# Spreading eight bias rows over 128 partitions in a decoder trunk: four skewed DRAM writes from SBUF against one DRAM to DRAM copy and one read

## The chip, the core and the metric

One core of one Trainium2 chip runs the whole program. The metric is the time of one execution in device microseconds (us); lower is better. The kernel before took 974.55 us, the median of three runs (974.48, 974.55 and 975.95).

## The reference

A two-layer decoder trunk over 256 tokens of width 1024. Each layer is a half-step SwiGLU feed-forward (width 2816), a mixer (differential attention, a short convolution and a gated recurrence side by side, one projection in and one out), and a second half-step feed-forward. Only one piece of it matters here, the relative bias of the attention:

```python
dist = q_pos[:, None] - k_pos[None, :]
bias = rel_bias[t5_bucket(jnp.maximum(dist, 0))]
...
logits = jnp.einsum('bqhmd,bkhmd->bhmqk', qb, k).astype(f32) + bias
logits = jnp.where(dist >= 0, logits, NEG_INF)
```

The bias of one of the eight maps (4 heads, 2 maps each) depends on the distance q - k alone. So a row of 384 numbers holds all of a map: row q of the bias is that row read from a place shifted by q.

## The kernel before, in words

All weights are float32 and are streamed from DRAM once, in 167 pieces of mostly 512 KB, in one fixed list. `load` (L143) issues a piece's DMA on SP into one of six `raw` buffers. `high` (L159) lets ScalarE (ACT) write the piece's float32r part `wh`, `low` (L164) lets VectorE (DVE) write the rest `wl`; `wh` and `wl` have seven buffers each. When `low` has freed a `raw` buffer, the next piece is loaded (`low_to`, L168). TensorE (PE) multiplies with `wh` and `wl` in three products (`mm3`, L203), which stand in the profile as L204, L205 and L206.

The first feed-forward runs `up_gate` (L300): 11 units (`c` from 0 to 10), each of four pieces and 48 matmuls of 128x512 into two PSUM banks `na` and `nb`. At the end of a unit `gate` (L313) lets ACT apply Silu (`sg`, L317) and DVE multiply (`ga`, L319). During the next unit `turn` (L324) transposes `ga` on PE (`hT`, four matmuls of L328), and ACT and DVE copy the result into `hid` (L330, L331). Then `ffn` (L374) runs the down projection (L221, L222) over 22 more pieces.

Each engine runs its instructions in the order in which they are written; a DMA is issued by the sequencer of the engine that it is written on, and what stands behind it there waits until the issue is through. At the end of a unit, after `gate`, `up_gate` calls a hook (L371). The dictionary `once` (L826 to L829) puts the setup of the mixer there:

- hook 1, `constants_in`: small loads on ACT's queue. Hook 2, `bias_rows` (L456): one matmul and a copy make `br`, 8 rows of 384 floats on 8 partitions of SBUF.
- hooks 3 to 6, `skew_out(0)` to `skew_out(3)` (L462): each writes two rows of `br`, each 128 times, into the DRAM scratch `skew`, laid out [8, 128, 384].
- hooks 7 to 10, `skew_in(0)` to `skew_in(3)` (L470): each reads two maps back into `bias` (128 partitions, 8, 256), partition p from an address that moves by 383 floats and not 384, which makes the shift. The first reader of `bias` is the attention of the mixer (L541), after the whole down projection.

The DMAs of SP and ACT share eight completion semaphores, DMAHW0 to DMAHW7, which are given out in turn in the order of the program. A DMA is issued only when the one before it on the same semaphore has landed. With hardly any DMAs but the loads, a load thus waits for the DMA written eight places before it.

Of the kernel before, what the change touches and what calls it, by code (L numbers as in the profile page):

```python
# [11 lines left out]
F32 = mybir.dt.float32  # L12
# [5 lines left out]
P = 128  # L18
DEPTH = 2
S = 256  # L20
# [50 lines left out]
def trunk(ctx: ExitStack, tc: tile.TileContext, t, out):  # L71
    nc = tc.nc
# [7 lines left out]
    dr = ctx.enter_context(tc.tile_pool(name="dr", bufs=1, space=bass.MemoryType.DRAM))  # L80
# [28 lines left out]
    bias = cst.tile([P, 8, S], F32, name="bias")  # L109
# [264 lines left out]
    def ffn(norm, first, gain, hooks=()):  # L374
        hid, last = up_gate(norm, first, hooks)
        for n in range(4):
            acc = pair("d")
            for k0, k1 in DOWN_K:
                w = take(1)[0]
                for i in range(2):  # L380
                    c = slice(i * P, (i + 1) * P)
                    for k in range(k0, k1):
                        wide(acc[i], w[0][:, k - k0, c], w[1][:, k - k0, c], hid[k], k == 0, k == KF - 1)
                    if k1 == KF:
                        settle(2 * n + i, acc[i], gain, True)
                done(1)
                if n == 0 and k0 == 8:
                    last()
                pump()


    kept = {}
# [66 lines left out]
        kept["br"] = wk.tile([8, 384], F32, tag="at", name="br")  # L459
        nc.vector.tensor_copy(out=kept["br"], in_=b[:8, :384])  # L460

    def skew_out(i):  # L462

        if i == 0:
            kept["skew"] = dr.tile([8, P, 384], F32, name="skew")
        m = slice(2 * i, 2 * i + 2)
        rows_ = kept["br"][m].unsqueeze(1).to_broadcast([2, P, 384])
        nc.scalar.dma_start(out=kept["skew"][m], in_=rows_)

    def skew_in(i):  # L470
        sk = kept["skew"][:]
        nc.scalar.dma_start(
            out=bias[:, 2 * i:2 * i + 2],
            in_=bass.AP(sk.tensor, sk.offset + 2 * i * P * 384 + P - 1, [[383, P], [P * 384, 2], [1, S]]),
        )


    def mixer(l, norm):
# [344 lines left out]
        nc.vector.tensor_tensor(out=xq, in0=junk[:, 0], in1=junk[:, 1], op=ALU.add)  # L823

    norm = Norm()
    once = {1: constants_in, 2: bias_rows, 3: exponents, 4: softplus, 5: factors}  # L826
    for i in range(4):
        once[3 + i] = (lambda i, old: lambda: (old and old(), skew_out(i)))(i, once.get(3 + i))
        once[7 + i] = lambda i=i: skew_in(i)  # L829
    ffn(norm, True, ("mix_norm", 0), once)  # L830
    for l in range(DEPTH):
        norm = Norm()
# [126 lines left out]
```

## Time and profile before

| what | value |
|---|---|
| median of three runs | 974.55 us |
| the profiled execution, whole | 974.53 us |
| its span (first to last instruction) | 972.4 us |
| PE busy in it | 956.2 us (98%) |
| DVE, ACT busy | 582.4 us (60%), 508.1 us (52%) |
| mean granted TensorE clock | 0.994 |
| moved by DMA | 176.64 MB, 171.46 MB of it on SP's queue (q1), 4.30 MB on ACT's (q10) |

The span is the sum to compare with; 2.1 us lie around it. Two of the page's lines, in 40 slices of 24.3 us each, show where the kernel is uneven: PEclk is the granted TensorE clock in tenths of full speed, and DMA the busy share of the 16 DMA engines in tenths.

| line | slices 0 to 39 |
|---|---|
| PEclk | 9999989999999999999999999999999999999999 |
| DMA | 8854465644346555555555455556434455555621 |

Slice 5 (121.6 to 145.9 us) is the only one with a clock digit under 9.

### The profile page before, as it was taken

The numbers are of one execution on the slowest core, as the hardware profiler recorded it, in microseconds if no ns is written. First come the engines' busy times: TensorE is split into PE (matmuls) and PEld (weight loads), VectorE is DVE, ScalarE is ACT, GpSimd is POOL, SyncE is SP. The second block draws the span as 40 slices with busy tenths as digits, with TensorE's granted clock in tenths as the row PEclk, the third lists the DMA queues.
The fourth block names the chain that finished last, engine by engine and source line by source line (L and its number), as shares of the span: only waits on it lengthen the run. The fifth ranks groups of instructions, "written<-read, shape, count | busy, mean of one in ns | idle before, by whom it ended". The sixth has DMA issues, their size and how long they took to land.

```text
span 972.4 us, 13915 instructions
## 1 busy us (share of the span) xinstructions
PE 956.2 (98%) x5350; PEld 831.9 (86%) x5350; DVE 582.4 (60%) x812; ACT 508.1 (52%) x775; POOL 24.1 (2%) x46
## 2 busy tenths in 40 slices
PE   9999889999999999999999999999999999999997
PEld 7788668899999888888888888888999988888886
DVE  6665355567787555555655555565778765555543
ACT  7564244457775554444445444454678655444441
POOL 0011000000000000000000000000000000000000
PEclk9999989999999999999999999999999999999999
DMA  8854465644346555555555455556434455555621
GB/s 307 292 181 150 155 238 186 205 164 163 131 174 206 189 200 183 178 172 188 174 215 179 174 189 183 163 188 222 160 136 161 163 210 197 176 174 189 220 89 44
DMA packets 53045, 176.64 MB, mean 182 GB/s; under 512 B 6867, under 2 KB 8948, under 8 KB 52980
## 3 DMA queue, kind: packets, MB, share of 16 engines
q1 hardware_dynamic: 48960, 171.46, 51.4%
q10 hardware_dynamic: 4020, 4.30, 1.5%
q8 instruction: 42, 0.69, 0.3%
q14 instruction: 23, 0.19, 0.1%
HBM read 173.11 MB, written 2.62 MB: 181 GB/s over the span
## 4 chain that ended last, share of the span: by engine, by line
PE 90%; DMA 7%; issue 1%; ACT 1%; DVE 1%; SPq 0%; ACTq 0%; POOLq 0%; POOL 0%; DVEq 0%
PE na L204 7%; PE nb L204 7%; PE na L206 7%; PE na L205 7%; PE nb L206 7%; PE nb L205 7%; PE db L221 6%; PE da L221 6%; DMA skew<-br 3%; DMA raw<-in_ffn_gu 3%; PE da L222 3%; PE db L222 3%; PE hT L328 2%; PE v L204 1%; PE wb L206 1%
## 5 line engine op out<-in xcount | busy, mean ns | idle before, releaser
L162 ACT ACTIVATE wh<-raw 128x1024 fp32r<-128x1024 f32 (+1 forms) x334 | 340.3, 1031 | 292.9 <-PE nb L206 102.8
L166 DVE TENSOR_TENSOR wl<-raw,wh 128x1024 fp32r<-128x1024 f32 (+1 forms) x334 | 388.5, 1187 | 77.9 <-ACT wh L162 77.9
L204 PE MATMUL na<-wh,xx 128*128 128x512 f32 x352 | 142.4, 404 | 0.6 <-ACT wh L162 0.6
L205 PE MATMUL na<-wl,xx 128*128 128x512 f32 x352 | 138.2, 393 | 0.2 <-DVE wl L166 0.2
L206 PE MATMUL na<-wh,xx 128*128 128x512 f32 x352 | 138.4, 393 | 0.0
L204 PE MATMUL nb<-wh,xx 128*128 128x512 f32 x352 | 137.8, 391 | 0.0
L206 PE MATMUL nb<-wh,xx 128*128 128x512 f32 x352 | 137.4, 390 | 0.0
L205 PE MATMUL nb<-wl,xx 128*128 128x512 f32 x352 | 137.2, 390 | 0.0
L331 DVE TENSOR_TENSOR hid<-hT,hid 128x512 fp32r<-128x512 f32 x44 | 30.4, 691 | 133.1 <-ACT hid L330 133.1
L221 PE MATMUL da<-hid,wh 128*128 128x512 f32 x252 | 92.3, 399 | 0.0
L221 PE MATMUL db<-hid,wh 128*128 128x512 f32 x252 | 92.1, 398 | 0.0
L206 PEld LDWEIGHTS na<-wh,xx 128*128 128x128 f32 x352 | 66.6, 189 | 14.4
L204 PEld LDWEIGHTS nb<-wh,xx 128*128 128x128 f32 x352 | 66.5, 189 | 13.9
L205 PEld LDWEIGHTS nb<-wl,xx 128*128 128x128 f32 x352 | 66.4, 189 | 14.0
L204 PEld LDWEIGHTS na<-wh,xx 128*128 128x128 f32 x352 | 66.8, 190 | 13.5 <-ACT wh L162 1.5
L206 PEld LDWEIGHTS nb<-wh,xx 128*128 128x128 f32 x352 | 66.2, 188 | 14.1
L205 PEld LDWEIGHTS na<-wl,xx 128*128 128x128 f32 x352 | 66.9, 190 | 13.0 <-DVE wl L166 0.8
L222 PE MATMUL da<-hid,wl 128*128 128x256 f32 x252 | 70.7, 280 | 0.0
L222 PE MATMUL db<-hid,wl 128*128 128x256 f32 x252 | 70.6, 280 | 0.0
L330 ACT ACTIVATE hid<-hT 128x512 fp32r<-128x512 f32 x44 | 26.3, 599 | 79.7 <-PE hT L328 79.7
L319 DVE SCALAR_TENSOR_TENSOR ga<-na,rr,sg 128x256 f32<-128x256 f32 x44 | 21.2, 483 | 76.7 <-ACT sg L317 76.7
L221 PEld LDWEIGHTS db<-hid,wh 128*128 128x128 f32 x252 | 47.4, 188 | 11.2
(282 smaller groups left out, 1520.8 us busy)
## 6 DMA issues: line engine op xcount, KB each, us to landing
raw<-in_ffn_gu SPq DMA_DIRECT2D x172, 512.0 KB, 4.4
raw<-in_ffn_down SPq DMA_DIRECT2D x82, 512.0 KB, 4.2
raw<-in_w_in SPq DMA_DIRECT2D x44, 512.0 KB, 4.5
raw<-in_w_out SPq DMA_DIRECT2D x16, 512.0 KB, 4.8
raw<-in_ffn_down SPq DMA_DIRECT2D x12, 256.0 KB, 2.7
raw<-in_ffn_gu SPq DMA_DIRECT2D x8, 256.0 KB, 5.5
skew<-br ACTq DMA_DIRECT2D x4, 384.0 KB
xT<-in_x SPq DMA_DIRECT2D x4, 256.0 KB, 5.7
```

What stands on the lines that cost most here:

```text
L162: nc.scalar.activation(out=parts[i][0][:, s], in_=raws[i][:, s], func=AF.Copy)
L166: nc.vector.tensor_tensor(out=lo[:, s], in0=raws[i][:, s], in1=h[:, s].bitcast(F32), op=ALU.subtract)
L204: nc.tensor.matmul(o, lhsT=ah, rhs=bh, start=first, stop=False)
L205: nc.tensor.matmul(o, lhsT=ah, rhs=bl, start=False, stop=False)
L206: nc.tensor.matmul(o, lhsT=al, rhs=bh, start=False, stop=last)
L221: nc.tensor.matmul(o, lhsT=wh, rhs=flat(v), start=first, stop=False)
L222: nc.tensor.matmul(o[:, :S], lhsT=wl, rhs=v[:, 0], start=False, stop=False)
L319: nc.vector.scalar_tensor_tensor(out=a[:, k], in0=b[k][:, 256:], scalar=norm.r[:, k:k + 1], in1=s[:, k], op0=ALU.mult, op1=ALU.mult)
L328: nc.tensor.transpose(b[:, (2 * j + k) * P:(2 * j + k + 1) * P], a[:, k, tok(j)], ident)
L330: nc.scalar.activation(out=h[:, :, 0], in_=two(b), func=AF.Copy)
L331: nc.vector.tensor_tensor(out=h[:, :, 1], in0=two(b), in1=h[:, :, 0].bitcast(F32), op=ALU.subtract)
```

## The change

The row buffer `br` goes out to a small DRAM buffer `rows` as it is (hook 6). A second DMA copies that buffer 128 times within DRAM into `skew`, now laid out [128, 8, 384] (hook 8). A third reads all of `bias` back at once, partition p from an address that moves by 8 x 384 - 1 floats (hook 10). All three stay on ACT's queue. Eight DMAs become three; hooks 7 and 9 are gone, and hooks 3, 4 and 5 keep only the arithmetic that they had.

```diff
-    def skew_out(i):
-
-        if i == 0:
-            kept["skew"] = dr.tile([8, P, 384], F32, name="skew")
-        m = slice(2 * i, 2 * i + 2)
-        rows_ = kept["br"][m].unsqueeze(1).to_broadcast([2, P, 384])
-        nc.scalar.dma_start(out=kept["skew"][m], in_=rows_)
-
-    def skew_in(i):
+    def rows_out():
+        kept["rows"] = dr.tile([8, 384], F32, name="rows")
+        nc.scalar.dma_start(out=kept["rows"], in_=kept["br"])
+
+    def skew_out():
+
+        kept["skew"] = dr.tile([P, 8, 384], F32, name="skew")
+        r = kept["rows"][:]
+        nc.scalar.dma_start(out=kept["skew"], in_=bass.AP(r.tensor, r.offset, [[0, P], [384, 8], [1, 384]]))
+
+    def skew_in():
         sk = kept["skew"][:]
-        nc.scalar.dma_start(
-            out=bias[:, 2 * i:2 * i + 2],
-            in_=bass.AP(sk.tensor, sk.offset + 2 * i * P * 384 + P - 1, [[383, P], [P * 384, 2], [1, S]]),
-        )
+        nc.scalar.dma_start(out=bias, in_=bass.AP(sk.tensor, sk.offset + P - 1, [[8 * 384 - 1, P], [384, 8], [1, S]]))
...
-    once = {1: constants_in, 2: bias_rows, 3: exponents, 4: softplus, 5: factors}
-    for i in range(4):
-        once[3 + i] = (lambda i, old: lambda: (old and old(), skew_out(i)))(i, once.get(3 + i))
-        once[7 + i] = lambda i=i: skew_in(i)
+    once = {
+        1: constants_in, 2: bias_rows, 3: exponents, 4: softplus, 5: factors, 6: rows_out, 8: skew_out, 10: skew_in
+    }
```

Three places show how the instructions move. The number behind a name only tells one buffer from another, and "waits" names the semaphores that an instruction waits for.

The first is ACT's queue at the end of unit 8. Before:

```order
L317 ACTIVATE sg<-na,rr 128x256
L317 ACTIVATE sg<-nb,rr 128x256
L472 DMA bias<-skew 128x2x256
L162 ACTIVATE wh_1070<-raw_959 128x1024 [waits DMAHW0_49,DVE_49,PE_49]
L330 ACTIVATE hid_124<-hT 128x2x256 [waits PE_49]
```

Now:

```order
L317 ACTIVATE sg<-na,rr 128x256
L317 ACTIVATE sg<-nb,rr 128x256
L470 DMA skew<-rows 128x3072 [waits DMAHW0_49]
L162 ACTIVATE wh_1067<-raw_956 128x1024 [waits DMAHW4_49,DVE_49,PE_49]
L330 ACTIVATE hid_124<-hT 128x2x256 [waits PE_49]
```

The read of two maps has given way to the copy within DRAM, which waits for the copy of `rows` that was issued two units earlier.

The second is ACT's queue at the end of unit 10, the last of `up_gate`. Before:

```order
L317 ACTIVATE sg<-nb,rr 128x256
L472 DMA bias<-skew 128x2x256
L162 ACTIVATE wh_1250<-raw_1135 128x1024 [waits DMAHW1_49,DVE_49,PE_49]
L162 ACTIVATE wh_1272<-raw_1162 128x1024 [waits DMAHW3_49,DVE_49,PE_49]
L330 ACTIVATE hid_125<-hT 128x2x256 [waits PE_49]
```

Now:

```order
L317 ACTIVATE sg<-nb,rr 128x256
L474 DMA bias<-skew 128x8x256 [waits DMAHW1_49]
L162 ACTIVATE wh_1246<-raw_1132 128x1024 [waits DMAHW5_49,DVE_49,PE_49]
L162 ACTIVATE wh_1268<-raw_1158 128x1024 [waits DMAHW6_49,DVE_49,PE_49]
L330 ACTIVATE hid_125<-hT 128x2x256 [waits PE_49]
```

One read of all eight maps stands there now; it waits for the copy within DRAM (DMAHW1), and the high parts of the next pieces and the last `hid` stand behind it.

The third is SP's queue, where a load takes over the semaphore of a slow DMA. Before, the loads written eight places behind the writes of `skew`:

```order
L151 DMA raw_773<-in_ffn_gu 128x1024 [waits DMAHW6_49,DVE_49]
L151 DMA raw_810<-in_ffn_gu 128x1024 [waits DMAHW7_49,DVE_49,Activation_49]
L151 DMA raw_835<-in_ffn_gu 128x1024 [waits DMAHW0_49,DMAHW1_49,DVE_49,Activation_49]
L151 DMA raw_853<-in_ffn_gu 128x1024 [waits DMAHW2_49,DVE_49]
L151 DMA raw_871<-in_ffn_gu 128x1024 [waits DMAHW3_49,DVE_49]
L151 DMA raw_898<-in_ffn_gu 128x1024 [waits DMAHW4_49,DMAHW5_49,DVE_49,Activation_49]
```

Now, the eighth load behind the copy within DRAM, which has DMAHW1 (with `raw_1219`):

```order
L151 DMA raw_1158<-in_ffn_down 128x1024 [waits DMAHW7_49,DVE_49,Activation_49]
L151 DMA raw_1183<-in_ffn_down 128x1024 [waits DMAHW0_49,DVE_49,Activation_49]
L151 DMA raw_1201<-in_ffn_down 128x1024 [waits DMAHW2_49,DVE_49]
L151 DMA raw_1219<-in_ffn_down 128x512 [waits DMAHW3_49,DMAHW1_49,DVE_49]
L151 DMA raw_1250<-in_ffn_down 128x1024 [waits DMAHW4_49,DVE_49,Activation_49]
```

The loads still wait for ACT's DMAs eight places back, but in the gate and up pieces of units 4 to 10 no write of `skew` stands there any more.

## Rows read from the trace of the kernel before

**Rows 1.** The page, busy time of each engine, its share and instructions.

```profile
PE 956.2 (98%) x5350; PEld 831.9 (86%) x5350; DVE 582.4 (60%) x812; ACT 508.1 (52%) x775; POOL 24.1 (2%) x46
```

**Rows 2.** Waits of PE, whole span: total us, times, longest us.

```profile
PE hT L328 <- DVE ga L319: 8.3, 3, 5.6
```

**Rows 3.** Timeline of PE: start us, us; in brackets idle before.

```profile
107.07 1.29 PE L328 MATMUL hT<-ident,ga 128*128 128x128 f32 x4 [2.33 <-DVE ga L319]
108.02 0.78 PE L204 MATMUL na<-wh,xx 128*128 128x512 f32 x1
...
126.03 1.29 PE L328 MATMUL hT<-ident,ga 128*128 128x128 f32 x4 [5.57 <-DVE ga L319]
126.97 0.78 PE L204 MATMUL na<-wh,xx 128*128 128x512 f32 x1
```

**Rows 4.** Chain that ended last, 30 to 240 us: start us, us, what.

```profile
70.69 0.44 PE hT L328 x4
...
76.77 33.27 DMA skew<-br
...
112.52 11.41 DMA raw<-in_ffn_gu
124.04 0.46 ACT wh L162
...
140.14 0.44 PE hT L328 x4
...
237.02 0.64 PE sc L539 x4
```

**Rows 5.** The same chain in the second feed-forward.

```profile
334.12 0.44 PE hT L328 x4
...
345.47 0.44 PE hT L328 x4
```

**Rows 6.** Windows: length, PE, PEld, DVE, ACT, POOL busy (count); PEclk; DMA share; GB/s.

```profile
87.00:92.00 5.00, 5.00 (x24) 4.14 (x23) 3.71 (x5) 1.79 (x3) 0.00 (x0) 1.00 0.11 29
...
102.00:107.00 5.00, 2.74 (x13) 1.93 (x11) 1.69 (x3) 2.85 (x4) 0.00 (x0) 1.00 0.13 51
107.00:112.00 5.00, 4.86 (x16) 3.89 (x17) 1.54 (x3) 0.00 (x0) 0.00 (x0) 0.66 0.26 59
...
127.00:132.00 5.00, 5.00 (x15) 4.00 (x14) 2.32 (x3) 1.15 (x2) 0.00 (x0) 0.57 0.69 232
132.00:137.00 5.00, 5.00 (x23) 4.13 (x22) 3.21 (x4) 3.36 (x5) 0.00 (x0) 1.00 1.03 412
...
905.00:910.00 5.00, 5.00 (x28) 4.32 (x27) 3.22 (x4) 2.84 (x4) 0.00 (x0) 1.00 0.87 305
```

**Rows 7.** Waits of SP's queue, 92 to 130 us: total us, times, longest us.

```profile
SPq L151 <- DMA skew<-br: 35.4, 3, 12.4
```

**Rows 8.** Timeline of SP, pieces around a pause in the loads.

```profile
81.31 0.33 SPq L151 DMA_DIRECT2D raw<-in_ffn_gu  x1
...
93.54 2.28 SPq L151 DMA_DIRECT2D raw<-in_ffn_gu  x2
```

**Rows 9.** Timeline of ACT (ACTq is its DMA issue): start us, us, [idle before].

```profile
57.44 0.75 ACTq L468 DMA_DIRECT2D skew<-br  x1
...
105.16 9.33 ACTq L472 DMA_DIRECT2D bias<-skew  x1
...
114.61 1.06 ACT L162 ACTIVATE wh<-raw 128x1024 fp32r<-128x1024 f32 x1 [7.75 <-PE na L206]
...
146.21 0.37 ACTq L472 DMA_DIRECT2D bias<-skew  x1
```

**Rows 10.** DMA issues: queue, count, KB each, median us to landing where known.

```profile
skew<-br ACTq DMA_DIRECT2D x4, 384.0 KB
...
bias<-skew ACTq DMA_DIRECT2D x4, 256.0 KB, 4.8
bd<-in_final_norm ACTq DMA_DIRECT2D x1, 512.0 KB
```

## The prediction

> **What bounds the kernel now.** I read the page first: PE is busy for 956.2 us of the 972.4 us span [rows 1], so time can only come from its idle time or from stretches in which it runs at the lower clock. The waits of PE name one idle group of any size, the transposes `hT` waiting for `ga`: 8.3 us in three waits, the longest 5.6 us [rows 2]. The timeline places two of them, 2.33 us before 107.07 and 5.57 us before 126.03, and shows that the four transposes behind each take 1.29 us and the next matmul 0.78 us [rows 3]. In the chain of waits four transposes that did not wait have a share of 0.44 us [rows 4, 5]. [...]
>
> What the two stalls and the slow stretches cost together is read from the chain. The transposes stand once per unit. Undisturbed units of the second feed-forward are 345.47 - 334.12 = 11.35 us apart [rows 5]. From 70.69 to 140.14 there are five units and 69.45 us [rows 4]; five times 11.35 are 56.75. So **12.70 us** are lost: 2.33 + 5.57 = 7.90 idle, and the other 4.80 at the lower clock behind it: 126.03 - 107.07 - 11.35 - 5.57 = 2.04 behind the first stall, 140.14 - 126.03 - 11.35 = 2.76 behind the second [rows 3, 4].
>
> Who is late? The chain goes back from the second stall over `wh` at 124.04 and a load that needed 11.41 us to a write of `skew`, 33.27 us from its issue at 76.77 to its landing at 110.04 [rows 4]. The waits of SP's queue say the same: its loads stood 35.4 us for `skew<-br`, in three waits [rows 7]. The place is the shared completion semaphore: the loads eight places behind the writes may not go out until these have landed. So SP issued nothing between 81.31 + 0.33 and 93.54, a pause of 11.9 us [rows 8]. In 87 to 92 us, when no load was under way, the DMA engines were 0.11 busy, 29 GB/s [rows 6]: 0.11 x 16 = 1.8 engines. The four writes, 4 x 384 KB = 1.573 MB, took from 57.44 [rows 9] to 110.04, or 52.6 us, 29.9 GB/s. They ran at the speed of two engines from the first to the last, and every load has a share on those two. ACT suffers as well: the first read of `bias` held its issue for 9.33 us, and the next `wh` started only at 114.61 [rows 9].
>
> **The change, part by part.**
>
> Removed: the four writes from two partitions. With them go the 35.4 us of SP's waits, the slow landing of loads beside them and the long issue at 105.16. The loads for units 4 to 10 then run as in the second feed-forward, whose units go at 11.35 us without a stall [rows 5]. Worth 12.70 us if nothing takes their place. Late next is nothing on the loads' side: the next thing a unit waits for is PE.
>
> Added, hook 6: `rows`, 12 KB from 8 partitions. It replaces an issue that took 0.75 us for the first write [rows 9], and has two units, 22.7 us, before the copy needs it. Nothing on the path; if it were late, ACT would stand at hook 8.
>
> Added, hook 8: the copy within DRAM, at about 146.21 - 12.70 - 2 x 11.35 = 110.8 us. The trace has none. Its size is 1.573 MB on each side, its outer step 128 long. Bounds: at the highest rate of the windows, 412 GB/s [rows 6], 3.8 us; at the rate of the present writes 52.6 us. Between them I take 16 engines at the speed that two showed, 29 / 2 x 16 = 232 GB/s, or **6.8 us**. The reason is the nearest row of its form: the load of `final_norm`, 128 times the same 4 KB of DRAM [rows 10], falls into 905 to 910 us, and the engines move 305 GB/s there, busy 0.87 [rows 6]. Reading the same bytes 128 times thus does not collect on few engines. [...]
>
> What could wait for the copy? Two things. The read at hook 10 waits for it on ACT, 22.7 us later; behind it stand the high parts of the next pieces and the last `hid`. And the eighth load behind it takes its semaphore; seven loads at 11.35 / 4 = 2.84 us pass first, 19.9 us. At 6.8 us neither waits, and the copy may take three times as long before one does. Cost: 0, covered by these 19.9 us.
>
> Added, hook 10: one read of 1.05 MB in place of four of 256 KB, which landed in 4.8 us each [rows 10]. It lies between 1.05 MB at 412 GB/s, 2.5 us, and four such landings in a row, 19.2 us; I take the middle, about 11 us. Its first reader is the attention at 237.02 [rows 4], some 91 us behind an issue at 133.5. An issue of a quarter of it took 0.37 us [rows 9]; four times that is 1.5 us of ACT's queue, which had 9.33 us to bear before. Cost: 0.
>
> Removed beside it: five issues on ACT, 0.37 to 0.75 us each where they did not wait [rows 9]. PE never waited for these; 0.
>
> Sum: 974.53 - 12.70 + 0 = **961.8 us**. The profiled execution stands 0.02 us under the median of 974.55, so the sum holds for it too.
>
> **The rivals.**
>
> A burst instead of a trickle. Copy and loads share the engines. If loads got nothing while the copy runs, the hole in them would be as long as the copy. Before, a pause of 11.9 us followed by slow landing emptied the buffers, and PE stood 2.33 us at the end [rows 8, 3]; 6.8 us are a little over half of it. If the copy takes 12 us or more and starves the loads, a stall like the first comes back: 2.33 + 2.04 = 4.4 us, **966.2 us**. For it speaks the size, three loads at once; against it that the engines have room, since the page's DMA line, shown with the profile before, reads mostly 4 to 6 tenths, and that my copy is some 5 us short of the point. I give it a tenth. [...]
>
> Slower than before: the copy goes at the speed of two engines, as the writes did. It then lands 52.6 us after 110.8, at 163.4. ACT stands at the read from 133.5 for 29.9 us. PE has the pieces already split, and goes on until the down projection wants the last two `hid`, five pieces or 14.2 us on; then it idles 15.7 us and loses some 2.4 us more at the lower clock: 961.8 + 18.1 = **980 us**. The turning point is where this eats the 12.70 us: a copy of about 47 us, 33 GB/s. Against it speaks that no repeated read from DRAM in the trace shows such a rate [rows 6], for it that each of the new steps waits for the one before.
>
> The change does not do what it seems to: the loss is not due to the two engines but to the amount written and read beside the loads, and returns in units 8 to 10 and in the down projection. Then about **974.5 us**, between 972.5 and 976.5. Against it: in 87 to 92 us the engines stood almost idle while SP waited [rows 6], so amount cannot have been the limit.
>
> **How the numbers follow.** The forecast has 0.84, the burst 0.10, the slow copy 0.03, no gain 0.03. The range takes in the forecast and the burst: from 960.8, one us below for what the units' spacing cannot tell (and since the runs before spread over 1.5 us), to 966.5. About 0.2% or 1.9 us is what a measurement of this kernel can tell from no change. Forecast and burst are faster by more than that: 0.94. No gain gives most of 0.03 to the same, the slow copy 0.03 to slower.
>
> **What the changed profile would show.** Right: `hT` once every 11.35 us from 70.69 on, the last but one at 127.4 in place of 140.14; PE's waits for `ga` down from 8.3 to some 0.4 us; no wait of SP for `skew`; granted clock 1.00 from 100 to 140 us; the copy landed within 20 us and the issue on ACT at hook 10 short. A span near 959.7 us. Wrong on the copy: ACT's issue at hook 10 stands for several us, or SP waits for `skew<-rows`. Wrong on the burst: a wait of `hT` or of a down matmul between 113 and 145 us. Wrong on the cause: stalls in units 7 and 8 though SP waits for no write.

## The result, and the profile after

The changed kernel took **961.97 us**, the median of four runs (961.24 to 962.83), against 975.25 us for the kernel before on the same occasions (974.48 to 976.4, four runs). The ratio is 0.9863 with a 95% interval of 0.9846 to 0.988: 13.3 us faster, where 12.70 were forecast. The forecast time was 961.8 us. The profiled execution took 961.27 us, with a span of 959.1 us.

The page of the changed kernel, first busy times and then the chain by engine, where DMA had 7% before:

```profile
PE 951.2 (99%) x5350; PEld 829.0 (86%) x5350; DVE 582.6 (61%) x812; ACT 508.2 (53%) x775; POOL 24.0 (3%) x46
...
PE 98%; issue 1%; DMA 0%; ACT 0%; DVE 0%; POOLq 0%; POOL 0%
```

PE's busy time fell by 5.0 us with as many matmuls [rows 1]: that is the stretch at the lower clock, which the windows of the kernel before give as 0.50 of full speed in 108 to 110 us and in 126 to 131 us. The rest is idle time. The waits of PE in the changed kernel (total us, times, longest us), in answer to [rows 2]:

```profile
PE warm L802 <- DVE ones L794: 1.0, 1, 1.0
PE na L204 <- ACT wh L162: 0.5, 1, 0.5
PE na L205 <- DVE wl L166: 0.2, 1, 0.2
```

`hT` no longer stands in the list at all. SP's queue waits for no write of `skew` either; in answer to [rows 7], 92 to 130 us, the largest group of its waits is the one for a free `raw` buffer:

```profile
SPq L151 <- DVE wl L166: 33.8, 13, 4.4
```

The windows of the changed kernel, the same stretches as in [rows 6] and the one in which the copy runs (columns as there):

```profile
87.00:92.00 5.00, 5.00 (x23) 4.14 (x23) 2.01 (x3) 2.85 (x4) 0.00 (x0) 1.00 0.70 229
...
102.00:107.00 5.00, 5.00 (x25) 4.15 (x24) 2.00 (x4) 1.93 (x3) 0.00 (x0) 1.00 0.34 109
107.00:112.00 5.00, 5.00 (x23) 4.13 (x22) 2.84 (x4) 2.85 (x4) 0.00 (x0) 1.00 0.81 264
112.00:117.00 5.00, 5.00 (x25) 4.14 (x24) 2.00 (x3) 2.23 (x3) 0.00 (x0) 1.00 1.01 355
```

PE is busy throughout, at a clock of 1.00. The copy and the loads together fill the 16 engines (1.01) for a few us, and nothing on PE shows it. The chain, in answer to [rows 4]:

```profile
69.96 0.44 PE hT L328 x4
...
126.70 0.44 PE hT L328 x4
```

Five units take 126.70 - 69.96 = 56.74 us, where they took 69.45. These 12.71 us are the forecast's term. Some 0.7 us more had been won by 70 us (69.96 against 70.69), in the start, where nothing was changed; the four runs of the changed kernel alone lie 1.6 us apart, so no cause is put on it. The new DMAs on ACT's queue:

```profile
110.08 0.58 ACTq L470 DMA_DIRECT2D skew<-rows  x1
...
132.78 0.40 ACTq L474 DMA_DIRECT2D bias<-skew  x1
```

Neither issue waits. And the size and landing of the copy, from the list of DMA issues:

```profile
skew<-rows ACTq DMA_DIRECT2D x1, 1536.0 KB, 8.7
```

The copy landed 8.7 us after its issue, against 6.8 forecast, well inside the 19.9 us that it had.

### The profile page after: what moved, and what is told of

Its sections match the earlier page's. It is cut to its first block, busy times and chain, and to the rows that moved or that the text cites. A ratio compares the mean times of both kernels' runs of the same rounds, so it can differ in the third digit from the quotient of the medians.

```text
span 959.1 us, 13905 instructions
## 1 busy us (share of the span) xinstructions
PE 951.2 (99%) x5350; PEld 829.0 (86%) x5350; DVE 582.6 (61%) x812; ACT 508.2 (53%) x775; POOL 24.0 (3%) x46
## 4 chain that ended last, share of the span: by engine, by line
PE 98%; issue 1%; DMA 0%; ACT 0%; DVE 0%; POOLq 0%; POOL 0%
PE na L205 8%; PE na L204 8%; PE nb L204 8%; PE na L206 8%; PE nb L206 8%; PE nb L205 8%; PE db L221 6%; PE da L221 6%; PE da L222 3%; PE db L222 3%; PE hT L328 2%; PE v L204 1%; PE wb L206 1%; PE wb L205 1%; PE wb L204 1%; PE wa L204 1%
## 5 line engine op out<-in xcount | busy, mean ns | idle before, releaser
L204 PEld LDWEIGHTS na<-wh,xx 128*128 128x128 f32 x352 | 66.2, 188 | 13.3 <-ACT wh L162 1.4
```

The lines of the kernel that those rows point to most:

```text
L204: nc.tensor.matmul(o, lhsT=ah, rhs=bh, start=first, stop=False)
```

## The experiments

The time came from the place that was foreseen. What was open is why the four writes were slow: the prediction held that their outer step of 2 put them on two DMA engines, and that 29 GB/s is what two engines move. The first four runs take that apart. Ratios are to the kernel before in the same runs, with 95% intervals.

### The same four transfers, from DRAM

```diff
+    def rows_out():
+        kept["rows"] = dr.tile([8, 384], F32, name="rows")
+        nc.scalar.dma_start(out=kept["rows"], in_=kept["br"])
...
-        rows_ = kept["br"][m].unsqueeze(1).to_broadcast([2, P, 384])
-        nc.scalar.dma_start(out=kept["skew"][m], in_=rows_)
+        r = kept["rows"][:]
+        src = bass.AP(r.tensor, r.offset + 2 * i * 384, [[384, 2], [0, P], [1, 384]])
+        nc.scalar.dma_start(out=kept["skew"][2 * i:2 * i + 2], in_=src)
...
+    once = {1: constants_in, 2: lambda: (bias_rows(), rows_out()), 3: exponents, 4: softplus, 5: factors}
```

> Four copies at hooks 3 to 6 and four reads at hooks 7 to 10 as before the change, but each copy reads its two rows from the DRAM buffer and not from two partitions of SBUF; the outer step of each is still 2 long. Theory (few engines: an outer step of 2 puts a transfer on two of the 16 DMA engines, whatever its source): the copies move about 30 GB/s, the four need some 50 us, SP's loads stand for skew by 30 us or more, PE waits for ga by about 8 us, and the time is that of the kernel before, 972 to 977 us. Rival (the source, two partitions of SBUF, was slow): each copy lands within 10 us, SP does not wait for skew, 961 to 963 us.

Measured: **962.35 us**, ratio 0.9866 (0.9852 to 0.9881), as fast as the changed kernel. Both theories were half right. A window of this run in which no load moved, and one of the kernel before:

```profile
99.00:102.00 3.00, 3.00 (x15) 2.49 (x14) 1.91 (x2) 1.34 (x2) 0.00 (x0) 1.00 0.13 50
```

```profile
88.00:92.00 4.00, 4.00 (x19) 3.32 (x18) 2.71 (x4) 1.79 (x3) 0.00 (x0) 1.00 0.11 25
```

The share is 0.13, 2.1 of 16 engines, so the copies did stay on two; but these two moved 50 GB/s. The write of before moved 25 alone: the 29 of [rows 6] hold the last 0.01 MB of a load, which landed between 87 and 88. So 29 GB/s was not the rate of two engines. SP's waits for `skew` were still there:

```profile
SPq L151 <- DMA skew<-rows: 26.7, 3, 10.8
```

26.7 us in place of 35.4 [rows 7], and PE did not idle in units 4 to 10: all its windows from 57 us on are full. The pieces already split carried PE over pauses of up to 10.8 us here, and did not over those of up to 12.4 us in [rows 7].

### One transfer from SBUF, on eight partitions

```diff
-    def skew_out(i):
+    def skew_out():
...
-        rows_ = kept["br"][m].unsqueeze(1).to_broadcast([2, P, 384])
-        nc.scalar.dma_start(out=kept["skew"][m], in_=rows_)
+        rows_ = kept["br"].unsqueeze(1).to_broadcast([8, P, 384])
+        nc.scalar.dma_start(out=kept["skew"], in_=rows_)
...
+    once = {1: constants_in, 2: bias_rows, 3: exponents, 4: softplus, 5: factors, 8: skew_out, 10: skew_in}
```

> One write of all eight rows from the eight partitions of SBUF at hook 8, no buffer of rows in DRAM, one read at hook 10. Theory (few engines): eight engines, 4 x 30 = 120 GB/s, so about 13 us to land; the loads share eight engines of 16 for that time, which the buffers cover: no wait of PE for ga, 961 to 963 us. Rival (a source in SBUF read 128 times is slow by itself): 50 us as the four writes took, ACT stands at hook 10 for some 30 us, 975 us or more.

Measured: **966.25 us**, ratio 0.9911 (0.989 to 0.9931); the theory of engines alone fails, and so do the rival's 50 us and 975 us. Windows of this run while the write was under way:

```profile
120.00:122.00 2.00, 2.00 (x11) 1.65 (x10) 2.00 (x3) 0.75 (x2) 0.00 (x0) 1.00 0.43 48
124.00:126.00 2.00, 2.00 (x10) 1.67 (x9) 0.14 (x2) 1.54 (x3) 0.00 (x0) 1.00 0.42 48
```

0.43 x 16 = 6.9 engines are busy, and all of them move only 48 GB/s, less than two engines did from DRAM. What was slow here lay on the side of SBUF. The read at hook 10 could be issued only when the write had landed:

```profile
149.47 0.45 ACTq L470 DMA_DIRECT2D bias<-skew  x1
150.05 2.00 ACT L162 ACTIVATE wh<-raw 128x1024 fp32r<-128x1024 f32 x2 [8.40 <-DMA skew<-br]
```

That is 36.3 us after the write's issue at 113.18. PE then waited 3.1 us for the last `hid`, in the profiled execution, which at 969.88 us was the slowest of the four.

### One copy within DRAM, on two engines

```diff
-        nc.scalar.dma_start(out=kept["skew"], in_=bass.AP(r.tensor, r.offset, [[0, P], [384, 8], [1, 384]]))
+        nc.scalar.dma_start(
+            out=bass.AP(sk.tensor, sk.offset, [[4 * 384, 2], [8 * 384, P], [1, 4 * 384]]),
+            in_=bass.AP(r.tensor, r.offset, [[4 * 384, 2], [0, P], [1, 4 * 384]]),
+        )
```

> The changed kernel, with its one copy within DRAM written as two halves of the maps, outer step 2, runs of 6 KB in place of 12 KB; same bytes, one DMA, same hooks. Theory (few engines): two engines. At the 30 GB/s of the writes before it takes 52 us, ACT stands at hook 10 for 30 us, SP's eighth load too, PE idles some 16 us: 976 to 982 us; if long runs go at the 26 GB/s per engine that loads reach, 30 us, ACT stands some 8 us and the time is 962 to 968 us. Rival (it is the number of DMAs, or that they stood two units earlier, that cost the 12.7 us): lands in about 9 us, 961 to 963 us.

Measured: **971.57 us**, ratio 0.9957 (0.994 to 0.9974), between the two branches. Two windows, of which the second has no load in it and the first 0.01 MB, and ACT at hook 10:

```profile
142.00:147.00 5.00, 5.00 (x33) 4.43 (x32) 0.00 (x0) 0.00 (x0) 0.00 (x0) 1.00 0.13 53
147.00:152.00 5.00, 1.48 (x9) 1.03 (x8) 0.00 (x0) 0.00 (x0) 0.00 (x0) 1.00 0.12 52
```

```profile
152.26 0.44 ACTq L477 DMA_DIRECT2D bias<-skew  x1
152.82 2.00 ACT L162 ACTIVATE wh<-raw 128x1024 fp32r<-128x1024 f32 x2 [16.93 <-DMA skew<-rows]
154.73 0.58 ACT L330 ACTIVATE hid<-hT 128x512 fp32r<-128x512 f32 x1
```

Two engines from DRAM: 52 GB/s with runs of 6 KB, 50 with runs of 1.5 KB. Beside the loads the copy needed 40.75 us (111.49 to its landing at 152.24 by the chain), where 1.573 MB at 52 GB/s are 30.2 us. ACT stood 16.93 us, and PE 7.6 us for the last `hid`. This is the rival "slower than before" of the prediction at a smaller size: the number of engines alone, with everything else as in the changed kernel, is worth 9.6 us. The busy share went with the outer step: 0.13 for a step of 2 here, 0.43 for the step of 8 in the write from eight partitions.

### No copy

```diff
...
-        sk = kept["skew"][:]
-        nc.scalar.dma_start(out=bias, in_=bass.AP(sk.tensor, sk.offset + P - 1, [[8 * 384 - 1, P], [384, 8], [1, S]]))
+        r = kept["rows"][:]
+        nc.scalar.dma_start(out=bias, in_=bass.AP(r.tensor, r.offset, [[0, P], [384, 8], [1, S]]))
...
```

> The copy within DRAM is left out, and the read at hook 10 takes unshifted rows, so the bias has the wrong shift. What is left shows what the copy costs. Theory (the copy is wholly hidden): the same as the changed kernel, 961 to 963 us, PE without a wait in the first feed-forward. Rival (the copy, 8.7 us of all 16 engines, still delays something): faster by 1 us or more, under 960.5 us.

Measured: **961.67 us**, ratio 0.9861 (0.9844 to 0.9878), the same as with the copy (0.9863). The copy costs nothing that can be measured; the intervals leave room for some 1.7 us either way.

### Rows four partitions apart

The four writes of the kernel before, but with the rows on partitions 0, 4, 8 to 28.

```diff
-        rb = sm.tile([NB + 1, 8], F32, tag="rb", name="rb", bufs=1)
+        rb = sm.tile([NB + 1, 32], F32, tag="rb", name="rb", bufs=1)
+        nc.vector.memset(rb, 0.0)
...
-        nc.scalar.dma_start(out=rb[:NB, :], in_=t["rel_bias"])
+        nc.scalar.dma_start(out=rb[:NB, 0:32:4], in_=t["rel_bias"])
...
-        rows_ = kept["br"][m].unsqueeze(1).to_broadcast([2, P, 384])
+        rows_ = kept["br"][8 * i:8 * i + 8:4].unsqueeze(1).to_broadcast([2, P, 384])
```

A first form of it spread the columns of `rb` by two steps on VectorE in hook 2, in place of by the load:

> The kernel before, with one thing changed: the eight rows stand on partitions 0, 4, 8 to 28 of SBUF and not on 0 to 7, so the two partitions that a write reads are four apart (two small steps on VectorE and a wider matmul put them there, under 1 us). Theory (neighbouring partitions share one way out of SBUF, whose some 29 GB/s was the rate of the four writes, below the 50 GB/s that two engines reached from DRAM): the rate beside no load goes from 29 to 45 to 55 GB/s, PE's waits for ga fall under 3 us, 962 to 965 us. Rival (each partition gives about 14.5 GB/s, or a source in SBUF is slow by itself): 29 GB/s and 973 to 977 us as before.

Measured: 969.11 us, ratio 0.9931 (0.9916 to 0.9946), between the two. The waits of PE tell why:

```profile
PE bt L461 <- issue: 4.2, 1, 4.2
```

The matmul that makes the rows started at 46.17, right behind the second of the two steps on VectorE, and these stood behind all that VectorE's queue held before them:

```profile
45.90 0.17 DVE L460 COPY rw<-rb 33x8 f32<-33x8 f32 x1
```

So 4.2 us of idle and the slow stretch behind it (matmuls 0.42 to 0.43 us apart from 48.34 to 50.90, 0.23 from 51.78 on) were my edit's, not the writes'. From 57 us on PE had no wait, and a window without a load shows 50 GB/s:

```profile
104.00:107.00 3.00, 3.00 (x15) 2.49 (x14) 2.14 (x2) 1.22 (x2) 0.00 (x0) 1.00 0.13 50
```

The same edit for the single write on eight partitions:

> One write of eight rows from SBUF at hook 8, as in the run from eight neighbouring partitions, which took 36 us and 966 us in all, but the rows stand on partitions 0, 4, 8 to 28. Theory (neighbours share a way out): the write lands in 8 to 13 us at 120 GB/s or more, ACT does not stand at hook 10, 961 to 963.5 us. Rival (eight engines or a repeated row in SBUF are slow by themselves): lands in some 36 us again, 965 to 968 us.

Measured: 968.03 us, ratio 0.9924 (0.9907 to 0.994), above the range for the same reason (3.6 us of idle at that matmul). But ACT did not stand at hook 10: the read was issued at 137.84, 22.71 us after the write at 115.13, which is the spacing of two units. So the write took at most 22.7 us, where from neighbouring partitions it took 36.3. Its landing is not among the issues of the trace, but its packets are: 1032 on ACT's queue (q10), eight more than the 1024 copies of a row. Those of this run all lie between 117.6 and 130.2 us, those of the run with neighbours between 115.5 and 149.1. The queue in these two windows, this run first (packets, MB, share of 16 engines):

```profile
q10 hardware_dynamic: 1032, 1.57, 33.3%
```

```profile
q10 hardware_dynamic: 1032, 1.57, 34.8%
```

1.57 MB in 12.6 us are 125 GB/s beside the loads, against 47: the rate that the theory gave. The landing, 15.1 us after the issue, came a little later than its 8 to 13.

The clean form, with the rows spread by the load as in the diff:

> As the run with the rows on partitions 0, 4 to 28 and four writes of two, but the rows are put there by the small load of the table itself, so VectorE has no step more that PE waits for (that cost 4.2 us of idle and some more at the lower clock). Theory (neighbouring partitions share one way out of SBUF): 50 GB/s beside no load, no wait of PE for ga over 2 us, 961.5 to 964 us. Rival (what the spread rows won had other grounds, such as the later start of the writes): PE waits for ga as in the kernel before, 970 us or more.

Measured: **962.54 us**, ratio 0.9866 (0.9848 to 0.9883). Beside the partitions only a small memset in hook 1 and the width of one matmul and its copy differ from the kernel before, and the whole loss is gone. A window of it without a load, and SP's waits:

```profile
98.00:101.00 3.00, 3.00 (x14) 2.47 (x14) 1.65 (x2) 1.34 (x2) 0.00 (x0) 1.00 0.13 50
```

```profile
SPq L151 <- DMA skew<-br: 26.7, 3, 10.7
```

### Rows 32 partitions apart

```diff
-        nc.scalar.dma_start(out=rb[:NB, :], in_=t["rel_bias"])
+        nc.scalar.dma_start(out=rb[:NB].rearrange("b (a c) -> b a c", a=2)[:, :, 0:4], in_=t["rel_bias"].rearrange("b (a i) -> b a i", a=2))
...
-        rows_ = kept["br"][m].unsqueeze(1).to_broadcast([2, P, 384])
-        nc.scalar.dma_start(out=kept["skew"][m], in_=rows_)
+        rows_ = kept["br"][i:i + 33:32].unsqueeze(1).to_broadcast([2, P, 384])
+        nc.scalar.dma_start(out=kept["skew"][i:i + 5:4], in_=rows_)
...
```

> The same with the rows on partitions 0 to 3 and 32 to 35, so that the two partitions of a write are 32 apart (maps 0 and 4, 1 and 5 and so on in one write and one read). If distance is what counts: 50 GB/s and 961.5 to 964 us, as with a distance of 4. [...]

Measured: **974.61 us**, ratio 0.9999 (0.999 to 1.0009): the kernel before again. The window answers to that of the kernel before from 88 us, shown above, and the waits answer to [rows 7] and [rows 2]:

```profile
88.00:92.00 4.00, 4.00 (x19) 3.34 (x18) 3.23 (x5) 1.34 (x3) 0.00 (x0) 1.00 0.11 26
```

```profile
SPq L151 <- DMA skew<-br: 35.6, 3, 12.3
```

```profile
PE hT L328 <- DVE ga L319: 8.1, 2, 5.4
```

So distance is not what counts. Two partitions that lie 32 apart moved 26 GB/s together, as two neighbours did with 25; two that lie four apart moved 50. That the slow pairs share a way out of SBUF agrees with these rates, but no view shows such a way by itself.

### The writes of before, further apart in time

```diff
-    for i in range(4):
-        once[3 + i] = (lambda i, old: lambda: (old and old(), skew_out(i)))(i, once.get(3 + i))
-        once[7 + i] = lambda i=i: skew_in(i)
+    once = {
+        1: constants_in, 2: lambda: (bias_rows(), skew_out(0)), 3: exponents, 4: lambda: (softplus(), skew_out(1)),
+        5: factors, 6: lambda: skew_out(2), 8: lambda: skew_out(3), 10: skew_in,
+    }
```

> The four writes of the kernel before, unchanged in form and source, but at hooks 2, 4, 6 and 8, two units apart and not one, and one read at hook 10. Theory (the rate of 29 GB/s costs only where writes follow one another faster than they land, 13.5 us each alone and some 20 beside loads, against 22.7 us between them): SP waits for skew by under 10 us, PE waits for ga by under 2 us, 961.5 to 965 us. Rival (any such write holds the loads up for good, spaced or not): PE waits as before, 970 us or more.

Measured: **961.51 us**, ratio 0.9857 (0.9843 to 0.9872). SP's waits for `skew` from 40 to 140 us:

```profile
SPq L151 <- DMA skew<-br: 3.7, 2, 2.5
```

The writes from neighbouring partitions on two engines did no harm here, with two units, 22.7 us, from one to the next. In the kernel before each was issued while an earlier one was still under way, the second at 65.44 us with packets of the first up to 75.86. (This edit also starts the writes one unit earlier and makes one read of four; what these two do by themselves was not tried.)

### A copy three times as large

```diff
-        kept["skew"] = dr.tile([P, 8, 384], F32, name="skew")
+        kept["skew"] = dr.tile([3 * P, 8, 384], F32, name="skew")
...
-        nc.scalar.dma_start(out=kept["skew"], in_=bass.AP(r.tensor, r.offset, [[0, P], [384, 8], [1, 384]]))
+        nc.scalar.dma_start(out=kept["skew"], in_=bass.AP(r.tensor, r.offset, [[0, 3 * P], [384, 8], [1, 384]]))
```

> The changed kernel with a copy within DRAM three times as large, 4.7 MB, at hook 8; only the first third is read. Theory (a burst on all engines is spread over all loads and the buffers hold it): at the 8.7 us for one, 26 us; ACT stands at hook 10 by some 3 us, SP's eighth load some 6 us, PE does not idle or under 2 us, 961.5 to 964 us. Rival (the burst starves the loads, from 12 us of copy on): a stall of PE of 2 us or more with the lower clock behind it, 966 us or more.

Measured: **961.36 us**, ratio 0.9854 (0.9839 to 0.9869).

```profile
skew<-rows ACTq DMA_DIRECT2D x1, 4608.0 KB, 22.7
```

4.72 MB in 22.7 us, from issue to landing, are 208 GB/s beside the loads. The loads came late enough for ACT to stand 4.35 us for one, at 133.26, but PE had no wait from 57 to 160 us. The prediction's rival "burst" put its turning point at a copy of 12 us; at nearly twice that PE still lost nothing.

## Why the prediction was right, and where not

**What bounded the kernel and the size of the loss: right.** The writes of `skew` were the cause, and the whole of the loss went: 12.71 us in the five units, against 12.70 read from the spacing of `hT`. Reading the loss from the spacing of undisturbed units, and not from the idle time alone, gave the 4.8 us at the lower clock too. That the clock was the lower one there is measured: 0.66 and 0.57 in [rows 6], and 0.50 in the narrower windows named above.

**SP's semaphores: a way of the delay, but not a measure of it, and not the only way.** With 26.7 us of such waits (the four copies from DRAM, and the rows four apart) PE lost nothing; with 35.4 it lost 12.7. The waits in the trace are not a loss that could be added up; only what the split pieces and the `raw` buffers cannot cover shows on PE, and where between 26.7 and 35.4 that starts was not tried. Two things more went with the slow writes. Loads landed late beside them, 11.41 us for the one in the chain [rows 4]. And ACT stood in three issues, 6.14 us at 76.77, 6.78 at 88.11 and 9.33 at 105.16; with the rows four apart, or from DRAM, an issue there took at most 1.02 us. Directly ahead of each stall the wait that ended last is one for a load, by ACT's high part in front of `sg`:

```profile
105.08 1.06 ACT L162 ACTIVATE wh<-raw 128x1024 fp32r<-128x1024 f32 x1 [0.74 <-DMA raw<-in_ffn_gu]
...
124.04 1.06 ACT L162 ACTIVATE wh<-raw 128x1024 fp32r<-128x1024 f32 x1 [0.75 <-DMA raw<-in_ffn_gu]
```

How much of the 12.7 us each of the three gave, no run separates.

**"They ran at the speed of two engines": wrong.** This was the step on the cause. They ran on two engines (0.11 x 16 = 1.8), but at the 25 GB/s that two neighbouring partitions gave alone. Two engines moved 50 GB/s from DRAM, and 50 from SBUF when their partitions lay four apart. A row of [rows 6] already spoke against the step: from 102 to 107 us, at the same share of two engines, 0.13, the kernel before moved 51 GB/s, 0.16 MB of loads beside 0.10 MB of a write. The second support, 1.573 MB in 52.6 us, was misread, and its 29.9 GB/s met 29 by luck. The write issued at 76.77 is the third of the four, so by 110.04 three had landed; SP's last pause for `skew`, 11.3 us, ends shortly before 127.70, and the last packet of the fourth write lies at 127.2. Three writes in 52.6 us are 22 GB/s, beside the loads. Three changes of the kernel before win all of it: another source, other partitions, or more time between the writes. "In one transfer" is not needed, and from SBUF it is not enough (966.25 us).

**The copy: right in its cost, low in its length.** 6.8 us were worked out as 16 engines at half of 29 GB/s each, and that premise fell with the step above. The packets of the copy lie between 112.4 and 118.5 us: it moved in 6.1 us, 258 GB/s, while 0.40 MB of loads passed beside it, and the other 2.4 of the 8.7 us lie between its issue and its first packet. So the estimate came near the time of moving by luck, and the time ahead of the first packet was left out. The cost of 0 holds, since leaving the copy out gave 0.9861 against 0.9863. The packets of the copy three times as large moved at 234 GB/s (4.72 MB between 112.5 and 132.7 us).

**The read: about 11 us taken, half of that measured.** Its landing is not among the issues of the trace, but its packets lie between 134.4 and 138.4 us, so it ended 5.6 us after its issue at 132.78. It cost nothing, as said.

**The rival "slower than before": right in kind, low per us.** By its formula a copy that lands 40.75 us after its issue costs 40.75 - 22.7 - 14.2 + 2.4 = 6.3 us; measured were 9.6. It left out what ACT still does between the read and the last `hid`: two high parts of 2.00 us together, the copies to `hid` and the way between them. From the read's issue at 152.26 to PE's next matmul at 156.09 these are 3.8 us, and 40.75 - 22.7 - 14.2 + 3.8 gives the 7.6 us that PE idled.

**The rival "burst": its turning point was too early,** as the copy of 22.7 us shows. It took a pause of SP's queue, in which no load could be issued at all, for the same as sharing the engines. That loads keep a share is shown by the 0.40 MB beside the copy.

## What to carry to other kernels

When a transfer is slow, ask two questions apart: how many DMA engines carry it (the busy share of a stretch in which no other queue moves a packet, times 16), and what each of them moves; many busy engines with few GB/s pointed here to the memory at one end (6.9 engines with 48 GB/s in the write from eight partitions). Rows that are read many times were better read here from DRAM (50 GB/s on two engines), or from partitions four apart (50), than from two neighbours (25), and the slow writes were harmless when 22.7 us lay between them. A DMA that shares semaphores with a stream of loads can hold the whole stream, though it uses two engines only: 35.4 us of SP's waits in [rows 7].

## What was not expected of the hardware

- Two neighbouring partitions, or two 32 apart, gave 25 and 26 GB/s together; two that are four apart gave 50; eight neighbours 48, and eight that are four apart 125 beside the loads.
- Two DMA engines moved 50 to 53 GB/s between DRAM tensors, so about 26 each, with runs of 1.5 KB as well as of 6 KB.
- 128 or 384 readings of the same 12 KB of DRAM went at 181 and 208 GB/s from issue to landing, beside the loads (1.573 MB in 8.7 us, 4.72 MB in 22.7 us; the 16 engines 1.01 busy from 112 to 117 us with the first, 0.89 to 1.13 from 112 to 132 us with the second).
- Two small steps on VectorE ahead of one matmul cost 4.2 us of PE's idle and some 6 us of the whole (ratio 0.9931 against 0.9866), while the copy of 1.5 MB within DRAM cost nothing.
